# First feed-forward of a hybrid decoder layer: group 1 by seven products, the left combinations kind by kind, twelve modulation sums moved

## The chip, the cores and the metric

The kernel runs on one core of one Trainium2 chip. The metric is device time in microseconds for one execution, the median of several runs. A run's time is a little longer than the span of its profile, which goes from the first to the last instruction.

## The reference

One layer of a decoder on 1024 tokens of width 1024, all in f32: a feed-forward half-step, a mixer (a short convolution beside a diagonal state-space model), a second feed-forward half-step, and a final norm. Each of the three sub-layers is normed and modulated by vectors that come from a condition:

```python
c_act = jax.nn.silu(cond)
mod = c_act @ w_mod[l] + b_mod[l]
(sh1, sc1, g1, sh2, sc2, g2, sh3, sc3, g3) = jnp.split(mod, N_MOD, axis=-1)

h = modulate(rms_norm(x, ffn1_norm[l]), sh1, sc1)
x = x + 0.5 * g1[:, None, :] * swiglu(h, ffn1_w_gate[l], ffn1_w_up[l], ffn1_w_down[l])
...                        # mixer with sh2, sc2, g2; second feed-forward with sh3, sc3, g3
def swiglu(h, w_gate, w_up, w_down):
    return (jax.nn.silu(h @ w_gate) * (h @ w_up)) @ w_down
```

The hidden width of a feed-forward is 2816. `w_mod` is 1024 x 9216, so each of the nine modulation vectors takes eight sums over 128 x 1024 tiles of weights. The state-space model needs tables (powers and sines of its parameters, products with its B and C matrices) that depend on weights alone, not on x.

## The kernel before, in words

**Tiling.** Activations lie with the model width on the 128 partitions, as tiles of 128 x 512: eight width tiles k for each of two token halves h. A product of f32 accuracy is made from three matmuls of a rounded high part and a low part of each operand (`mm3`, line 315). A weight tile or an activation tile is split into its two parts by a cast on ACT (high) and a subtraction on DVE (low): `Weights.pump` for weights, `split_act` (line 328) for activations.

**Groups.** The 2816 hidden columns of the first feed-forward are worked in eleven groups of 256, named fa0 to fa10 in the profile. Each group computes silu(gate) * up for both token halves and keeps the result in DRAM (`kept`), and the down projection follows in chunks of four groups (fad0, fad1) and a last part of three groups (fald).

**Two ways to do a group.** Group 0 is interleaved with the norm at the start. Group 1 (`gate_up`, line 1317) is plain: two gate and two up weight tiles, each against eight width tiles and two halves. Groups 2 to 10 (`seven`, line 626) see a group as a 2 x 2 block product and do it with seven block products instead of eight, in the manner of Strassen and Winograd. Each of the seven takes one left block (A11, S1, S2, S4, S3, A12, A22, where A's rows are the token halves and the S are sums and differences of blocks, so 4 tiles of 128 x 512 each) and one right block (a weight, or a sum of weights). The products are accumulated in three PSUM banks B, C, A for the gate side and three for the up side; partial results are copied out of them by ACT and added by DVE between the products. Here a group's plain order of products is `SEVEN`.

**Weights.** `Weights` (line 108) streams weights through three raw buffers and a ring of four split tiles. The sums of weights are made in the raw buffers by DMAs issued from POOL that add a second block onto the first (`add`, line 165). `Weights.seven` (line 147) fixes in which order the seven right-hand tiles are made (granules) and in which order they are used.

**Left combinations.** `combos1` (line 1258) makes S1, S3, S2, S4 of the normed x once, in place in the x tiles, one k after another, and splits them. The split of S4 waits for `left_free`, which is set inside group 1, because its tiles take the place of A21, which plain group 1 still reads. When the combinations are done the x tiles are given back, and the tables' pools take their place.

**Side work and the clock.** A counter (`Clock`, line 57) ticks once per `mm3`, 0.68 us of TensorE. Every `period` ticks it takes one step of a queue of side work, `side1` (line 1283): the left combinations, then `ssm_base` (line 1024, the base of the tables, 35 steps), then `ssm_batch` (line 1165) for each of eight batches of tables. A batch reads parameters, builds its tables on DVE, runs small matmuls and transposes (kp and tp), and stores the tables by DMA. If side work isn't finished when group 10 begins, the rest is driven out at that place in the program; then the tables' pools are closed and x is loaded again into that space.

**Modulation sums.** After the start, 56 sums (`mod_tile`, line 459) are still to be made, each of one 512 KB load issued on SP and one DVE operation over 128 x 1024 (in the profile wm<-wm,cact). `MODS = (12, 12, 20, 12)` shares them out: 12 in group 1, 12 in batches 4 to 7 of the tables (`gate1`, line 1247, three in a batch), 20 in the last part of the down projection, 12 in the mixer. The loads go round a small ring: 2 buffers for those in the batches, and each sum starts the load of another.

**What sets the order.** The program's text gives each instruction its priority. A planner with costs of its own then lays out the queue of each engine, taking the first instruction in text order that it thinks is ready, and allotting buffers as they come free. So an instruction can be issued long before its place in the text. On the chip each queue runs in the planned order, and an instruction that waits holds up all that stands behind it on its engine. At the start alone the order is written out by hand.

Of the kernel before, what the change touches and what calls it, by code (L numbers as in the profile page):

```python
# [28 lines left out]
NGRP = NF // 2  # L29
# [2 lines left out]
CH = 16  # L32
TAU = 8

SEVEN_FROM = (2, 1)

CHUNKS = 2

# [2 lines left out]
NB = 8  # L41
# [78 lines left out]
class Weights:  # L120
# [23 lines left out]
    def plain(self, src):  # L144
        self.order.append(self.granule(self.source(src)))

    def seven(self, b, inner=()):

        b11, b12, b22, b21 = (b[q] for q in range(4))
        x = self.source(b11)  # L150
        got = [self.granule(x, b12)]
        self.order.append(got[0])
        for src in inner:
            self.plain(src)
        y = self.source(b12, b22)
        got += [self.granule(y, b11), self.granule(x), self.granule(y, b21)]
        got += [self.granule(self.source(src)) for src in (b22, b21)]
        got.append(self.granule(y))
        self.order.extend(got[q] for q in (2, 3, 4, 1, 5, 6))
# [62 lines left out]
def hymba_layer(ctx: ExitStack, tc, x_d, xt_d, wm1_d, wmod_d, gu1_d, gs1_d, ds1_d, wl1_d, win_d, wout_d, glu_d, gu2_d, gs2_d, wd2_d, ds2_d, wl2_d, cols_d, cond_d, lam_d, bc_d, out_d):  # L222
# [57 lines left out]
    def stream(gu, gs, wd, ds, wl, m):  # L280


        for g in range(m):
            plain([gu[2 * g], gu[2 * g + 1]])
        for g in range(m, NGRP):
            ws.seven(gs[g - m], [wd[:, q, :] for q in range(2)] if g == 1 else ())
        for c in range(CHUNKS):
            for p in range(2):
                ws.seven(ds[c, p])
        plain([wl[i] for i in range(wl.shape[0])])  # L290
# [332 lines left out]

    SEVEN = (("A11", "B"), ("S1", "C"), ("S2", "B"), ("S4", "C"), ("S3", "B"), ("A12", "A"), ("A22", "B"))

    def seven(name, between=None, kept=None, then=None):


        a_tiles, gate_, bank, t1, c1, u2 = {}, {}, {}, {}, {}, {}

        def copied(dst, b, side, nm):
            dst[side] = t2k(f"{name}{side}{nm}")
            A.copy(dst[side][:], bank[b, side][:])

        def add(dst, b, side):
            V.tensor_tensor(out=dst[side][:], in0=dst[side][:], in1=bank[b, side][:], op=ALU.add)

        def out(side, h, fi, src, t):
            if side == "g":
                A.activation(t[:], src[:], AF.Silu, scale=-1.0 if fi else 1.0)  # L640
                gate_[h, fi] = t
            elif kept is None:
                joined(t[:], src[:], gate_[h, fi][:], ALU.mult, fi == 1)
                a_tiles[fi, h] = split_act(t[:], f"{name}_{fi}_{h}a")
            else:
                keep(kept, f"A{h + 1}{fi + 1}", src[:], gate_[h, fi][:], ALU.mult, name, t[:], fi == 1)

        for n, (left, b) in enumerate(SEVEN):
            (w,) = ws.take()
            for half, side in enumerate("gu"):  # L650
                opens = (b, side) not in bank
                if opens:
                    bank[b, side] = ps(f"{name}{side}{b}")
                for k in range(4):
                    while len(blocks[left]) <= k:
                        clock.step()
                    mm3(bank[b, side][:], w, 4 * half + k, blocks[left][k], opens and k == 0, k == 3, more=not opens)
                if n == 0:
                    copied(t1, "B", side, "t1")
                elif n == 1:  # L660
                    copied(c1, "C", side, "c1")
                elif n == 2:
                    copied(u2, "B", side, "u2")
                elif n == 3:
                    add(u2, "C", side)
                    out(side, 0, 1, u2[side], u2[side])
                elif n == 4:
                    add(c1, "B", side)
                    out(side, 1, 1, c1[side], c1[side])
                elif n == 5:  # L670
                    add(t1, "A", side)
                    out(side, 0, 0, t1[side], t1[side])
                else:
                    if side == "g":
                        last = pools["first"].tile([P, HALF], F32, tag="first", name=f"{name}c21") if "first" in pools else acc_in_mov(f"{name}c21")
                    out(side, 1, 0, bank["B", side], last)
            ws.free()
            if n == 0 and between is not None:
                between()
            if then is not None:  # L680
                then(left)
        if kept is not None and kept.sums:
            keep_sums(kept, name)
            keep_last(kept, name)
        return a_tiles
# [479 lines left out]
    def ssm_batch(b):  # L1165
# [26 lines left out]
        bl = bt(f"bl{b}")  # L1192
        bl4 = bl[:, :512].rearrange("p (g n c) -> p g n c", g=GB, n=8)
        yield from comb(bl4, 8, (e1, e2), (bb[:, 0], bb[:, 1]), ALU.add, f"blt{b}")
        if b >= NB - 4:
            yield from gate1()

        def v3(a):
# [26 lines left out]
        tp = sm([P, 512], f"tp{b}")  # L1225
        for g in range(GB):
            T.transpose(tp[:, g * P : (g + 1) * P], bl[:, g * P : (g + 1) * P], ident[:])
        if b >= NB - 4:
            yield from gate1()
            yield from gate1()  # L1230
        kc = bt(f"kc{b}")
# [15 lines left out]
    def gate1():  # L1247

        if fetched:
            mod_tile(mod_home)  # L1250
            yield
# [1 line left out]
    def mod_home(name):  # L1253
        return mod_home.pool.tile([P, 1024], F32, tag="wm", name=name, bufs=2)[:]

    left_free = []

    def combos1():

        blocks.clear()  # L1260
        blocks.update(A11=act1[0][:4], A12=act1[0][4:], A22=act1[1][4:], S1=[], S2=[], S3=[], S4=[])
        for k in range(4):
            (t11, t21), (t12, t22) = x[k], x[4 + k]
            V.tensor_tensor(out=t22, in0=t22, in1=t21, op=ALU.subtract)
            blocks["S1"].append(split_act(t22, f"h1S1_{k}", "B"))
            yield
            V.tensor_tensor(out=t21, in0=t11, in1=t21, op=ALU.subtract)
            blocks["S3"].append(split_act(t21, f"h1S3_{k}", "B"))
            yield
            joined(t11, t22, t11, ALU.subtract, True)  # L1270
            blocks["S2"].append(split_act(t11, f"h1S2_{k}", "B"))
            yield
            joined(t12, t12, t11, ALU.subtract, True)
            yield
        while not left_free:
            yield
        for k in range(4):
            blocks["S4"].append(split_act(x[4 + k][0], f"h1S4_{k}", "A"))
            yield
        xp_open.close()  # L1280
        first_opened()

    def side1():
        yield from combos1()
        sb = side_open.enter_context(tc.tile_pool(name="sb", bufs=1, side="right"))
        with tc.tile_pool(name="sb1", bufs=1, side="right") as sb1:
            yield from ssm_base(sb, sb1)
# [26 lines left out]
        if d == KT - 1:  # L1314
            norm_into(act2, h, n2[h], 1, "h2")

    def gate_up(act, name, kept, last):

        afs = {}
        for fi in range(2):  # L1320
            if last and fi:
                wg, wu = ws.take(2)
                for h in (1, 0):
                    pg, pu = proj(wg, act[h], f"{name}g{fi}_{h}"), proj(wu, act[h], f"{name}u{fi}_{h}")
                    gu_keep(fi, h, pg, pu, afs, kept, name)
                    if h:
                        left_free.append(True)
                        clock.period = LAST_PERIOD
                ws.free(2)
                continue  # L1330
            (wg,) = ws.take()
            pg = [proj(wg, act[h], f"{name}g{fi}_{h}") for h in range(2)]
            ws.free()
            (wu,) = ws.take()
            for h in range(2):
                gu_keep(fi, h, pg[h], proj(wu, act[h], f"{name}u{fi}_{h}"), afs, kept, name)
            ws.free()

    movs["B"] = es1.enter_context(tc.tile_pool(name="movB1", bufs=12))
    LAST_PERIOD, BATCH_PERIOD = 2, 5.5  # L1340
    first_open = ExitStack()

    def first_opened():
        pools["first"] = first_open.enter_context(tc.tile_pool(name="first", bufs=1))

    MODS = (12, 12, 20, 12)

    share[0] = MODS[0]
    for _ in range(3):
        mod_fetch(mod_mov)  # L1350
    for i in range(MODS[0]):
        clock.after(2.5 * i + 3, lambda: mod_tile(mod_mov))
    clock.side.append(side1())
    clock.period = 3.5
    for g in range(1, SEVEN_FROM[0]):
        gate_up(act1, f"fa{g}", kept[g], g == SEVEN_FROM[0] - 1)
    clock.period = 4.5
    lefts = [{left: [] for left, _ in SEVEN} for _ in range(CHUNKS)]
    a_last = [{} for _ in LAST[0]]
    HOMES = dict(A11="A", S2="B", A12="A", S3="B", S1="B", A22="A", S4="A")  # L1360
# [12 lines left out]

    for g in range(SEVEN_FROM[0], NGRP):
        if g == NGRP - 1:
            while clock.side:
                clock.step()
            side_open.close()
            first_open.close()
            open_x(ctx)  # L1380
            load_x(range(2), (0, 2))
        if g == NGRP - 2:
            pools.pop("first")
        seven(f"fa{g}", kept=kept[g], then=(lambda left: fetch_chunk(0, left)) if g == NGRP - 1 else None)
    down7("fad0", lefts[0], 0, lambda left: fetch_chunk(1, left), lambda left: load_x(range(2), (1, 3)) if left == "A12" else None)
    down7("fad1", lefts[1], 0, fetch_last)
    clock.period = 4
# [456 lines left out]
```

## Time and profile before

| | |
|---|---|
| time, median of 3 runs | 1702.88 us (1699.06 to 1704.96) |
| time of the profiled execution | 1695.99 us |
| its span | 1694.2 us |
| TensorE busy / VectorE / ScalarE / GpSimd | 98% / 63% / 40% / 10% |
| group 1 (plain) begins / group 2 begins | 75.66 us / 119.18 us |
| group 10 begins / down chunk 0 begins | 442.03 us / 480.11 us |
| modulation loads | 56 of 512 KB, 6.6 us to landing |

In the profile PE is TensorE, DVE VectorE, ACT ScalarE, POOL GpSimd, and SPq the queue of SyncE, which issues most DMAs. An entry reads "result<-operands", with buffer numbers left out: h is an activation of the first norm, h1S a left combination, w a split weight, raw a loaded weight, wm a modulation weight, kp and tp the small products of a table batch, fa2uC the PSUM bank C of the up side of group 2. In brackets stand the idle time before an instruction and what ended it.

### The profile page before, as it was taken

Reading aid. Unit: us, or ns where it says so; the run is one execution under the profiler, and the core shown is the slowest. Engines: PE = TensorE matmul, PEld = TensorE weight load, DVE = VectorE, ACT = ScalarE, POOL = GpSimd, SP = SyncE. Lnnn points to the kernel's source line nnn. Section 1 sums busy time; section 2 is a strip of 40 time slices with the busy share of each in tenths; the row PEclk is TensorE's granted clock in tenths of the full one; section 3 lists DMA queues with packets and bytes.
Section 4 is the critical chain, followed back from the end, with each engine's and each line's share of the span. In section 5 each row is a group of like instructions: output and inputs, shape, how many; then the busy total and the mean of one; then the engine's idle time right before and its main releaser. Section 6 shows DMA issues by size and latency. Waiting matters only on the chain.

```text
span 1694.2 us, 20669 instructions
## 1 busy us (share of the span) xinstructions
PE 1664.0 (98%) x7545; PEld 1370.0 (81%) x7545; DVE 1063.2 (63%) x1572; ACT 670.3 (40%) x983; POOL 165.2 (10%) x203
## 2 busy tenths in 40 slices
PE   8999999999999999999999999999999999999997
PEld 5887878788878888788888778888888888888887
DVE  7976676776566767735666847856555655454454
ACT  7526333333454432332214416434444444322234
POOL 1001000001001102200000121000001001000003
PEclk9999999999999999999999999999999999999999
DMA  9557897887887768235753323557787777989812
GB/s 361 177 164 187 227 265 213 219 210 200 276 275 202 209 177 291 73 101 161 209 156 113 100 99 143 132 136 222 237 234 204 221 219 219 321 272 343 255 60 100
DMA packets 128552, 338.11 MB, mean 200 GB/s; under 512 B 22337, under 2 KB 37953, under 8 KB 127426
## 3 DMA queue, kind: packets, MB, share of 16 engines
q1 hardware_dynamic: 112898, 280.16, 47.7%
q0 software_dynamic: 15552, 56.63, 19.3%
q8 instruction: 59, 0.97, 0.2%
q14 instruction: 43, 0.35, 0.1%
HBM read 252.32 MB, written 76.02 MB: 194 GB/s over the span
## 4 chain that ended last, share of the span: by engine, by line
PE 80%; DVE 8%; DMA 7%; ACT 2%; issue 1%; SPq 1%; POOL 0%; DVEq 0%; POOLq 0%; ACTq 0%
PE fald L111 4%; DMA wm<-in_wmod 3%; PE p L111 3%; PE fbd_1B L111 3%; PE fbd_0B L111 3%; PE fb10d L111 2%; PE fad_0B L111 2%; PE fad_1B L111 2%; PE wo L111 2%; PE b L111 2%; PE u L111 2%; PE fad_1C L111 1%; DMA swx<-X 1%; PE fbd_1C L111 1%; PE fbd_0C L111 1%
## 5 line engine op out<-in xcount | busy, mean ns | idle before, releaser
L111 DVE TENSOR_TENSOR w<-raw,w 128x1024 fp32r<-128x1024 f32 x239 | 292.5, 1226 | 248.3 <-ACT w L111 237.2
L111 ACT CAST w<-raw 128x1024 fp32r<-128x1024 f32 x239 | 250.9, 1051 | 305.0 <-DMA raw<-in_ds 59.4
L166 POOL DMA_DIRECT2D raw<-in_gs x76 | 66.7, 878 | 753.5 <-DVE w L111 425.9
L111 DVE CUSTOM_DVE_ANT_0 wm<-wm,cact 128x1024 f32<-128x1024 f32 x56 | 75.7, 1374 | 38.6 <-DMA wm<-in_wmod 38.6
L166 POOL DMA_DIRECT2D raw<-in_ds x32 | 28.0, 875 | 284.4 <-DVE w L111 162.5
L111 PE MATMUL p<-h,w 128*128 128x512 f32 x192 | 49.4, 407 | 1.7 <-ACT h L111 1.5
L111 PE MATMUL wo<-oa,w 128*128 128x512 f32 x192 | 46.7, 399 | 2.2 <-ACT w L111 2.2
L111 PE MATMUL wo<-ob,w 128*128 128x512 f32 x192 | 45.7, 392 | 1.1 <-ACT ob L111 0.6
L111 PE MATMUL v<-h,w 128*128 128x512 f32 x192 | 46.0, 393 | 0.0
L111 PE MATMUL c<-h,w 128*128 128x512 f32 x192 | 46.0, 393 | 0.0
L111 PEld LDWEIGHTS wo<-oa,w 128*128 128x128 f32 x192 | 36.9, 193 | 10.5 <-ACT w L111 2.6
L111 PE MATMUL b<-h,w 128*128 128x512 f32 x192 | 45.1, 392 | 0.0
L111 PE MATMUL u<-h,w 128*128 128x512 f32 x192 | 44.7, 391 | 0.2 <-DVE h L111 0.2
L111 PEld LDWEIGHTS p<-h,w 128*128 128x128 f32 x192 | 35.7, 192 | 9.9 <-ACT h L111 2.0
L111 PEld LDWEIGHTS wo<-ob,w 128*128 128x128 f32 x192 | 35.7, 188 | 9.3 <-ACT ob L111 1.0
L111 PEld LDWEIGHTS u<-h,w 128*128 128x128 f32 x192 | 35.7, 188 | 8.3 <-DVE h L111 0.6
L111 PEld LDWEIGHTS b<-h,w 128*128 128x128 f32 x192 | 35.7, 188 | 7.3
L111 PEld LDWEIGHTS v<-h,w 128*128 128x128 f32 x192 | 35.5, 188 | 7.1
L111 PEld LDWEIGHTS c<-h,w 128*128 128x128 f32 x192 | 35.5, 188 | 7.0
L111 DVE SCALAR_TENSOR_TENSOR x<-fb10d,gate,x 128x512 f32<-128x512 f32 (+1 forms) x20 | 12.9, 643 | 24.4 <-PE fb10d L111 24.3
L111 PE MATMUL fb10d<-fb9lA,w 128*128 128x512 f32 (+1 forms) x120 | 25.6, 347 | 0.0
L111 DVE TENSOR_TENSOR X<-co,X 128x512 f32<-128x512 f32 x8 | 5.5, 693 | 31.5 <-DMA swx<-X 24.7
(1503 smaller groups left out, 3868.5 us busy)
## 6 DMA issues: line engine op xcount, KB each, us to landing
raw<-in_gs SPq DMA_DIRECT2D x76, 512.0 KB, 4.8
raw<-in_gs POOLq DMA_DIRECT2D x76, 512.0 KB, 6.4
wm<-in_wmod SPq DMA_DIRECT2D x56, 512.0 KB, 6.6
raw<-in_ds SPq DMA_DIRECT2D x32, 512.0 KB, 4.9
raw<-in_ds POOLq DMA_DIRECT2D x32, 512.0 KB, 7.6
mw<-in_wm SPq DMA_DIRECT2D x8, 1024.0 KB, 8.3
raw<-in_win SPq DMA_DIRECT2D x16, 512.0 KB, 4.3
raw<-in_gu SPq DMA_DIRECT2D x12, 512.0 KB, 9.8
```

Of the source, the lines that this page charges most:

```text
L111: r = getattr(self.engine, name)(*args, **kw)
L166: self.G.dma_start(out=r[:], in_=src, accum_op=ALU.add)
```

## The change

Group 1 is done by seven products like groups 2 to 10, but in its own order `SOON`: A11 and A12 first, then S1, S2, S4, S3, A22. `Weights.seven` gets a matching order of loads and uses (`soon`). The left combinations are made kind by kind (all four S1, then S2, S4, S3), with no wait for plain group 1. The sums of group 1 are gone from there: batches 2 to 7 of the tables now take four each, 24 in all. The periods of the side work change: 2 ticks from group 1's start, 4.5 as soon as the combinations are done; in the batches it stays at 5.5.

```diff
-SEVEN_FROM = (2, 1)
+SEVEN_FROM = (1, 1)
...
-    def seven(self, b, inner=()):
+    def seven(self, b, inner=(), soon=False):
         b11, b12, b22, b21 = (b[q] for q in range(4))
+        if soon:
+            x, y = self.source(b11), self.source(b12, b22)
+            z = self.source(b21)
+            got = [self.granule(x, b12), self.granule(y, b11), self.granule(z), self.granule(x), self.granule(y, b21)]
+            got += [self.granule(self.source(b22)), self.granule(y)]
+            self.order.extend(got[q] for q in (0, 2, 3, 4, 5, 1, 6))
+            return
...
+    SOON = [SEVEN[n] for n in (0, 5, 1, 2, 3, 4, 6)]
+
-    def seven(name, between=None, kept=None, then=None):
+    def seven(name, between=None, kept=None, then=None, order=SEVEN):
...
-        for n, (left, b) in enumerate(SEVEN):
+        for n, (left, b) in enumerate(order):
...
-                    while len(blocks[left]) <= k:
+                    while len(blocks.get(left, ())) <= k:
                         clock.step()
...
-        if b >= NB - 4:
+        if b >= 2:
             yield from gate1()
...
-        if b >= NB - 4:
+        if b >= 2:
+            yield from gate1()
             yield from gate1()
             yield from gate1()
...
     def combos1():
...
             blocks["S1"].append(split_act(t22, f"h1S1_{k}", "B"))
             yield
+        for k in range(4):
+            (t11, t21), (t12, t22) = x[k], x[4 + k]
             V.tensor_tensor(out=t21, in0=t11, in1=t21, op=ALU.subtract)
-            blocks["S3"].append(split_act(t21, f"h1S3_{k}", "B"))
-            yield
             joined(t11, t22, t11, ALU.subtract, True)
             blocks["S2"].append(split_act(t11, f"h1S2_{k}", "B"))
             yield
+        for k in range(4):
+            (t11, t21), (t12, t22) = x[k], x[4 + k]
             joined(t12, t12, t11, ALU.subtract, True)
-            yield
-        while not left_free:
+            blocks["S4"].append(split_act(t12, f"h1S4_{k}", "A"))
             yield
         for k in range(4):
-            blocks["S4"].append(split_act(x[4 + k][0], f"h1S4_{k}", "A"))
+            blocks["S3"].append(split_act(x[k][1], f"h1S3_{k}", "B"))
             yield
         xp_open.close()
         first_opened()
 
     def side1():
         yield from combos1()
+        clock.period = 4.5
...
-    def gate_up(act, name, kept, last):
...
-    LAST_PERIOD, BATCH_PERIOD = 2, 5.5
+    BATCH_PERIOD = 5.5
...
-    MODS = (12, 12, 20, 12)
-
-    share[0] = MODS[0]
-    for _ in range(3):
-        mod_fetch(mod_mov)
-    for i in range(MODS[0]):
-        clock.after(2.5 * i + 3, lambda: mod_tile(mod_mov))
+    MODS = (0, 24, 20, 12)
+
     clock.side.append(side1())
-    clock.period = 3.5
-    for g in range(1, SEVEN_FROM[0]):
-        gate_up(act1, f"fa{g}", kept[g], g == SEVEN_FROM[0] - 1)
-    clock.period = 4.5
+    clock.period = 2
...
-        seven(f"fa{g}", kept=kept[g], then=(lambda left: fetch_chunk(0, left)) if g == NGRP - 1 else None)
+        seven(f"fa{g}", kept=kept[g], order=SOON if g == 1 else SEVEN, then=(lambda left: fetch_chunk(0, left)) if g == NGRP - 1 else None)
```

More of the change, by code (lines that the diff above doesn't have):

```diff
@@ L285, in stream @@
         for g in range(m, NGRP):
-            ws.seven(gs[g - m], [wd[:, q, :] for q in range(2)] if g == 1 else ())
+            ws.seven(gs[g - m], [wd[:, q, :] for q in range(2)] if g == 1 and wd is not None else (), g == 1 and wd is None)
         for c in range(CHUNKS):
@@ L654, in seven @@
                 for k in range(4):
-                    while len(blocks[left]) <= k:
+                    while len(blocks.get(left, ())) <= k:
                         clock.step()
                     mm3(bank[b, side][:], w, 4 * half + k, blocks[left][k], opens and k == 0, k == 3, more=not opens)
-                if n == 0:
+                if left == "A11":
                     copied(t1, "B", side, "t1")
-                elif n == 1:
+                elif left == "S1":
                     copied(c1, "C", side, "c1")
-                elif n == 2:
+                elif left == "S2":
                     copied(u2, "B", side, "u2")
-                elif n == 3:
+                elif left == "S4":
                     add(u2, "C", side)
                     out(side, 0, 1, u2[side], u2[side])
-                elif n == 4:
+                elif left == "S3":
                     add(c1, "B", side)
                     out(side, 1, 1, c1[side], c1[side])
-                elif n == 5:
+                elif left == "A12":
                     add(t1, "A", side)
@@ L1254, in mod_home @@
         return mod_home.pool.tile([P, 1024], F32, tag="wm", name=name, bufs=2)[:]
-    left_free = []
     def combos1():
@@ L1315, in after1 @@
             norm_into(act2, h, n2[h], 1, "h2")
-    def gate_up(act, name, kept, last):
[L1319 to L1337, printed above, removed]
     movs["B"] = es1.enter_context(tc.tile_pool(name="movB1", bufs=12))
-    LAST_PERIOD, BATCH_PERIOD = 2, 5.5
+    BATCH_PERIOD = 5.5
     first_open = ExitStack()
```

## The prediction

> **What bounds the kernel now.** I read the page's busy shares and chain first, then a table of windows with one row for each group of the first feed-forward, then the waits of TensorE in that stretch.
>
> ```profile
> span 1694.2 us, 20669 instructions
> PE 1664.0 (98%) x7545; PEld 1370.0 (81%) x7545; DVE 1063.2 (63%) x1572; ACT 670.3 (40%) x983; POOL 165.2 (10%) x203
> PE 80%; DVE 8%; DMA 7%; ACT 2%; issue 1%; SPq 1%; POOL 0%; DVEq 0%; POOLq 0%; ACTq 0%
> ...
> L111 DVE TENSOR_TENSOR w<-raw,w 128x1024 fp32r<-128x1024 f32 x239 | 292.5, 1226 | 248.3 <-ACT w L111 237.2
> ```
>
> TensorE is busy 98% of the span and carries 80% of the chain, so matmuls taken out count in full unless a wait takes their place. The windows below go from the first matmul of group 1 to that of group 2, and so on; the one from 442.00 is group 10, the one from 480.11 the first down chunk. Columns: length, then busy us of PE, PEld, DVE, ACT, POOL, granted clock, DMA share, GB/s.
>
> ```profile
> 75.66:119.18 43.52, 43.52 (x194) 36.04 (x192) 30.73 (x70) 9.67 (x14) 3.61 (x36) 1.00 0.72 211
> 119.18:158.96 39.78, 38.96 (x169) 31.30 (x168) 29.25 (x67) 25.10 (x43) 3.53 (x4) 1.00 0.60 144
> 158.96:197.04 38.08, 38.08 (x169) 31.53 (x168) 20.03 (x30) 12.76 (x17) 3.52 (x4) 1.00 0.81 219
> 197.04:236.74 39.70, 38.79 (x170) 31.54 (x169) 30.06 (x45) 12.01 (x17) 3.52 (x4) 1.00 0.91 277
> 236.74:278.02 41.28, 41.28 (x193) 33.55 (x193) 31.50 (x58) 15.56 (x23) 3.52 (x4) 1.00 0.79 210
> 278.02:321.63 43.61, 41.83 (x193) 33.39 (x193) 32.39 (x57) 15.49 (x24) 3.53 (x4) 1.00 0.80 212
> ...
> 402.50:442.00 39.50, 39.50 (x181) 32.42 (x180) 21.73 (x31) 14.95 (x20) 3.54 (x4) 1.00 0.79 215
> 442.00:480.11 38.11, 38.11 (x169) 31.53 (x168) 21.52 (x29) 19.79 (x31) 3.52 (x4) 1.00 0.99 334
> 480.11:560.00 79.89, 76.52 (x328) 62.18 (x327) 55.86 (x75) 41.50 (x65) 7.04 (x8) 0.98 0.82 236
> ```
>
> ```profile
> PE fad_1C L111 <- ACT fad_1c L111: 2.9, 1, 2.9
> PE fa6gB L111 <- DVE fa6gc L111: 1.0, 1, 1.0
> PE fa4uB L111 <- DVE fa4uc L111: 0.8, 1, 0.8
> PE fa6uB L111 <- DVE fa6uc L111: 0.8, 1, 0.8
> ```
>
> A group by seven products without table batches takes 38.08 us (group 3). A batch adds its kp and tp matmuls: group 5 holds two and takes 41.28, so 1.60 each, with no wait. Against this, group 2 loses 39.78 - 38.08 = 1.70 us, group 4 1.62, group 6 43.61 - 41.28 = 2.33. These three and the losses in the first down chunk are all that the stretch has to give or to grow.
>
> **Group 1: fewer matmuls.** By plain products it has 192 matmuls, by seven 7 x 2 x 4 x 3 = 168.
>
> ```profile
> 75.66 11.04 PE L111 MATMUL fa1g<-h,w 128*128 128x512 f32 x48
> 113.74 5.60 PE L111 MATMUL fa1u<-h,w 128*128 128x512 f32 x24
> 119.18 2.88 PE L111 MATMUL fa2gB<-h,w 128*128 128x512 f32 x12
> ```
>
> It runs without a gap, 0.2267 us a matmul. 24 fewer are **-5.44 us**, and group 1 becomes a 38.08.
>
> What that group gets on the other engines: three more weight tiles to split (DVE 1.23 each by the page's group; ACT 1.0, two in 2.01 in a row below), six copies out of PSUM and six adds. For DVE that is 3.7 + 6 x 0.68 (an operation of that size, below) = 7.8 us more, but ten of the twelve modulation sums that leave lie inside its window, 12.3 us of its 30.73. All this lies beside 38 us of matmuls; if this cover were gone it would cost its own 7.8.
>
> **Left combinations.** The new order needs A11 at 75.66, A12 at 81.10, then S1 at 86.54, S2 at 91.98, S4 at 97.42, S3 at 102.86. Before, three of the four kinds are made during the start, in gaps:
>
> ```profile
> 57.64 1.66 ACT L111 CAST h1S<-x 128x512 fp32r<-128x512 f32 x3
> 66.01 2.01 ACT L111 CAST w<-raw 128x1024 fp32r<-128x1024 f32 x2
> ```
>
> ```profile
> 69.87 1.21 DVE L111 CUSTOM_DVE_ANT_0 wm<-wm,cact 128x1024 f32<-128x1024 f32 x1
> 83.71 0.68 DVE L111 TENSOR_TENSOR h1S<-x,h1S 128x512 fp32r<-128x512 f32 x1
> ```
>
> The twelfth tile is done at 84.4, behind four sums (from 69.87 on) that go away. Kind by kind the four S1 tiles come first, so they have some 15 us in hand, and S4 (its buffers come free when A21 is last read, at 75.66) has 20. The first weights are cast by 68. I cost this at **0**; the cover is A11 and A12, 10.9 us of matmuls, and without it the price would be the wait for S1.
>
> **Four accumulating DMAs on POOL** join the weights of group 1. One falls in the start, where the DMA engines are full up to 40 us and then idle:
>
> ```profile
> 20.00:40.00 20.00, 19.61 (x91) 15.43 (x90) 16.77 (x28) 17.13 (x27) 6.71 (x5) 0.94 0.96 391
> 40.00:60.00 20.00, 20.00 (x105) 16.50 (x104) 18.64 (x31) 13.22 (x21) 0.00 (x0) 1.00 0.36 116
> ```
>
> 512 KB at 391 GB/s is 1.3 us, the upper bound if it pushed the last first-norm modulation load; I take 0, because after 40 us two thirds of the DMA time is free. The others have 10 us (two products) between the slot that comes free and the use.
>
> **The table base** (sines, powers: 25.10 us of ACT in group 2 against 12.76 in group 3) follows the combinations, whose end is seen by the load of its parameters:
>
> ```profile
> 109.74 0.33 SPq L111 DMA_DIRECT2D lam<-in_lam  x1
> ```
>
> It can start some 25 us earlier, in group 1. There the PSUM copies on ACT meet it as they now do in group 2. So the 1.70 moves with it: **0**, between -1.7 (it fits between) and +1.7 (both groups hit).
>
> **The sums.** All 24 now stand in batches 2 to 7, four in each, where 12 stood in batches 4 to 7. The order in program text isn't the order of issue: the planner pulls a sum forward as soon as it thinks its load has landed.
>
> ```profile
> 189.85 1.23 DVE L111 CUSTOM_DVE_ANT_0 wm<-wm,cact 128x1024 f32<-128x1024 f32 x1 [2.80 <-DMA wm<-in_wmod]
> 216.70 1.23 DVE L111 CUSTOM_DVE_ANT_0 wm<-wm,cact 128x1024 f32<-128x1024 f32 x1 [5.55 <-DMA wm<-in_wmod]
> 221.61 1.23 DVE L111 CUSTOM_DVE_ANT_0 wm<-wm,cact 128x1024 f32<-128x1024 f32 x1 [0.40 <-DMA wm<-in_wmod]
> 225.63 1.23 DVE L111 CUSTOM_DVE_ANT_0 wm<-wm,cact 128x1024 f32<-128x1024 f32 x1 [2.78 <-DMA wm<-in_wmod]
> 230.64 1.23 DVE L111 CUSTOM_DVE_ANT_0 wm<-wm,cact 128x1024 f32<-128x1024 f32 x1 [0.84 <-DMA wm<-in_wmod]
> 242.70 1.23 DVE L111 CUSTOM_DVE_ANT_0 wm<-wm,cact 128x1024 f32<-128x1024 f32 x1 [0.92 <-DMA wm<-in_wmod]
> 313.38 0.29 DVE L111 TENSOR_TENSOR bb<-prm,qq 128x128 f32<-128x128 f32 x1 [3.59 <-DMA si_d<-rott]
> ```
>
> Twelve sums stand between 189.85 and 243.9, long before batches 4 to 7. In group 4 DVE is busy 30.06 us and waits 5.55 + 0.40 + 2.78 + 0.84 = 9.57 for their loads: 39.63 of 39.70, DVE was the bound there, and behind each waiting sum stand the adds that free PSUM (fa4uc, 0.8 on PE) and the next weight split. Two buffers go round through SP, which holds weight loads behind them. Another twelve make a second such group: **+1.62**. Bounds: 0 if they fall into gaps, and 14.3 us if all their waits come through to PE (9.57 x 12 / 8 for the same spacing, as eight to nine sums lie in group 4).
>
> **Thinner batches.** Group 6 loses 2.33 where DVE waits 3.59 for a table to leave its buffer, with batches 5 steps (27.5 ticks of 0.68 us, and 1.60) apart. From batch 2 on they come 9 steps apart, 35.3 us. Batches 0 to 2 stay dense and now meet sums; I take half of it back, **-1.17** (bounds -2.33 and 0).
>
> **The end of the tables.** Before: 35 steps of 4.5 ticks for the base and 52 of 5.5 for the batches, 443 of the 448 ticks of groups 2 to 9. After: from tick 34 of group 1, 34 + 157.5 + 64 x 5.5 = 543 of 504. Some 7 steps, nearly all of batch 7, are driven out in one go before group 10. There the loads of x wait for the tables' space:
>
> ```profile
> 423.54 1.05 PE L111 MATMUL kp<-cl,bl 128*16 128x128 f32 x8
> ```
>
> ```profile
> 426.24 5.27 SPq L111 DMA_DIRECT2D mk_d<-kc  x8
> 435.05 0.82 SPq L111 DMA_DIRECT2D x<-in_x  x2
> ```
>
> x goes out 11.5 us after batch 7's kp, 7 us ahead of group 10. With kp at the group's start it goes out 11.5 us into it, 18.5 later. Its first use is in the fourth product of the down stage, over 50 us on, so x isn't late itself; what is late next is the fetches of kept tiles, in a group whose DMA engines are at 0.99. Three 512 KB loads more in it are 1.57 MB / 334 GB/s = 4.7 us of DMA. I take a third, **+1.5**, since most fetches are issued 20 us and more ahead; bounds 0 and 4.7, and -5.9 if the new order happens to spare the down chunk its present losses (below).
>
> **Sum:** -5.44 + 0 + 0 + 1.62 - 1.17 + 1.5 = **-3.5 us**. The profiled execution took 1695.99 us (span 1694.2 and 1.8 around it), so 1692.5 for one like it; the median shown is 6.9 above it, and by that 1702.88 - 3.5 = **1699.4**.
>
> **A rule on waits.** The largest wait of the stretch ends here:
>
> ```profile
> 503.30 1.23 PE L111 MATMUL fad_1C<-fa1lS,w 128*128 128x512 f32 x3 [2.93 <-ACT fad_1c L111]
> 507.75 0.85 PE L111 MATMUL fad_0B<-fa1lS,w 128*128 128x512 f32 x3
> ...
> 562.16 0.84 PE L111 MATMUL fad_0B<-fa5lA,w 128*128 128x512 f32 x3
> ```
>
> Twelve matmuls between the first two took 4.45 us instead of 2.72: after 2.93 us of idling the clock was down, 1.73 more. The down chunk (from 480.11; two passes of 38.08 would end at 556.27, but the next chunk, the third row, begins at 562.16) loses 5.89 in all. The Trainium skill, "TensorE: Matmul & The Clock Gate", Part 1, says that the clock halves only after an idle window of about 3.4 us and needs as long a busy one to come back. By the row, a new wait of three microseconds costs nearly five; by that rule one of 2.93 may cost only itself, and the third rival below would then be at 1702.1 instead of 1703.8. The trace decides for the row.
>
> **Rivals.**
> - *Clean.* The sums hide, group 6 and half of the down chunk's losses go: -5.44 - 2.33 - 2.9 = -10.7, **1692.2**. For it: DVE has 17 to 18 us free in each of groups 3, 9 and 10. Against: the loads, not DVE time, were the limit in group 4.
> - *Slower: DVE runs over.* In groups 4 to 6 sums, batches 0 to 2 and group work meet; from where DVE's busy time and its waits for modulation loads pass the group's 38 to 41 us, each further wait is PE's. All waits of the second twelve through: -5.44 + 14.3 = +8.9, **1711.7**. For it: group 4 stood at 39.63 of 39.70 with one table batch around it; groups 5 and 6 are at 31.5 and 32.4 without a sum. Against: only 1.62 of 9.57 came through, and the planner counts DVE's time, if not the loads'.
> - *Late fetches.* The down chunk's 5.89 doubles: -5.44 + 1.62 - 1.17 + 5.89 = +0.9, **1703.8**. For it: 0.99 of DMA. Against: the slack of the fetches.
> - *The change doesn't do what it says*: a late S1 or weight gives the 5.44 back in group 1, **1702.9**. Only the 15 us in hand speak against it.
>
> **How the numbers follow.** 0.3% is 5.1 us, about what a measurement can tell from no change. Forecast 0.42 (same 0.33, faster 0.09, since its own range is 1696.5 to 1702), clean 0.32 (faster 0.30, same 0.02), DVE over 0.12 (slower 0.11), late fetches 0.10 (same 0.06, slower 0.04), group 1 stalls 0.04 (same 0.03, slower 0.01). Together faster 0.39, same 0.45, slower 0.16. The range goes from a little under the clean case to short of the DVE case: 1690.5 to 1706.5.
>
> **What would show it.** Group 1 right: from its first matmul to group 2's 38 to 40 us, PE never ending a wait for h1S. The base: ACT-heavy in that window. Sums: 24 of them closing by about 290 us, with one or two groups at 39.7. Tables: batch 7's kp in the first matmuls of group 10, x behind it. The prediction is wrong if group 1 stays above 41 us, if the groups 3 to 9 together lose over 8 us, or if the sums stay in batches 2 to 7 as written and cost nothing.

## The result, and the profile after

The changed kernel takes **1691.07 us** (median of six, 1685.42 to 1692.94) against 1700.97 us for the kernel before, run beside it (1698.63 to 1705.86): a ratio of 0.9932, 95% interval 0.9917 to 0.9946. A second set of the same two kernels gave 0.9929 (0.9909 to 0.9949). By these ratios the change saves 11.6 and 12.1 us (the medians lie 9.9 and 11.2 apart), over three times the 3.5 forecast. The profiled execution took 1691.52 us. The page of the changed kernel, its span and busy line:

```profile
span 1689.7 us, 20647 instructions
PE 1657.2 (98%) x7521; PEld 1364.8 (81%) x7521; DVE 1065.5 (63%) x1581; ACT 676.8 (40%) x992; POOL 169.4 (10%) x207
```

24 matmuls are gone, three weight splits and four POOL DMAs have come. The table of windows, changed kernel, again one row for a group: group 1 (75.92), 2, 4, 5, 6, 7, 10 (440.49), and the first down chunk (478.67). Columns as before: length, then busy us of PE, PEld, DVE, ACT, POOL, granted clock, DMA share, GB/s.

```profile
75.92:114.02 38.10, 38.10 (x169) 31.52 (x168) 30.62 (x67) 15.23 (x21) 4.66 (x37) 1.00 0.63 145
114.02:152.10 38.08, 38.08 (x169) 31.53 (x168) 22.62 (x54) 25.04 (x43) 3.53 (x4) 1.00 0.76 197
...
190.18:229.86 39.68, 39.68 (x181) 32.54 (x180) 26.07 (x40) 12.18 (x18) 3.54 (x4) 1.00 0.90 275
229.86:275.92 46.06, 41.67 (x193) 33.48 (x192) 33.55 (x60) 15.50 (x23) 2.75 (x4) 1.00 0.78 221
275.92:316.10 40.18, 40.10 (x181) 32.38 (x180) 30.89 (x56) 14.39 (x21) 4.33 (x5) 1.00 0.90 255
316.10:359.69 43.59, 41.52 (x182) 33.62 (x180) 34.04 (x60) 15.41 (x22) 3.53 (x4) 0.96 0.86 241
...
440.49:478.67 38.18, 38.18 (x172) 31.62 (x170) 22.45 (x34) 21.70 (x34) 3.53 (x4) 1.00 0.96 304
478.67:555.45 76.78, 76.71 (x338) 62.91 (x336) 54.64 (x76) 40.42 (x62) 7.04 (x8) 1.00 0.92 269
```

What TensorE waited for from group 1 to the end of the down projection, changed kernel (total, times, longest):

```profile
PE kp L111 <- DVE bl L111: 3.3, 1, 3.3
PE fa7gB L111 <- DVE fa7gc L111: 2.1, 1, 2.1
PE fa5gC L111 <- DVE w L111: 1.1, 1, 1.1
```

Three things are to be seen. Group 1 takes 38.10 us in place of 43.52 and waits for nothing. Groups 2 to 9 still lose time, now in 5, 6 and 7: 46.06 - 41.28 (two batches) = 4.78 in group 5, 40.18 - 39.68 = 0.50 and 43.59 - 39.68 = 3.91, 9.2 in all. And the down chunk, where the largest wait of the kernel before stood, is nearly free: 76.78 against 82.05, where 76.16 is what its matmuls need.

The table below is the same reading for each kernel run here: the length of group 1, what groups 2 to 9 lose against 38.08 us and 1.60 for each batch whose kp lies in them, what down chunk 0 loses against 76.16, and the measured ratio to the kernel before (95% interval).

| kernel | group 1 | groups 2-9 lose | chunk 0 loses | ratio |
|---|---|---|---|---|
| before | 43.52 | 5.5 | 5.9 | 1 |
| before, again | 43.52 | 9.1 | 7.5 | 1 |
| after | 38.10 | 9.2 | 0.6 | 0.9932 (0.9917-0.9946) |
| after, again | 38.14 | 5.5 | 0.2 | 0.9929 (0.9909-0.9949) |
| before, x behind fetches | 43.52 | 9.1 | 0.3 | 0.9967 (0.9951-0.9982) |
| after, x early | 38.22 | 6.2 | 7.0 | 0.9960 (0.9947-0.9974) |
| after, x early but behind | 38.09 | 5.3 | 0.0 | 0.9937 (0.9919-0.9955) |
| before, sums moved | 43.52 | 8.2 | 7.6 | 1.0021 (1.0010-1.0032) |
| after, half the sums | 38.21 | 2.6 | 2.0 | 0.9924 (0.9910-0.9938) |
| after, usual order | 38.08 | 13.5 | 2.7 | 0.9994 (0.9982-1.0006) |
| after, sums held | 38.11 | 0.6 | 14.3 | 0.9969 (0.9955-0.9984) |
| held, batches 1-6 | 38.13 | 0.0 | 9.4 | 0.9943 (0.9928-0.9957) |
| the same, x behind | 38.16 | 0.0 | 10.5 | 0.9948 (0.9934-0.9962) |
| the same, 5 ticks a step | 38.12 | 0.0 | 1.7 | 0.9898 (0.9882-0.9914) |

Each trace is of one execution out of several: with the sums held it is the slowest of twelve (1700.44 us, median 1694.12), in the usual order the fastest of twelve, and in the last row the fastest of five (1679.88, median 1684.27), so the losses of these rows are not those of a median run.

With the means of the two traces of each kernel: group 1 gives -5.4, groups 2 to 9 give 7.35 - 7.3 = 0, chunk 0 gives 0.4 - 6.7 = -6.3. Their sum, -11.7, is the measured gain, but the match is closer than the method: the whole spans of the same four traces lie only 9.6 apart on average, because what follows chunk 0 is 1.9 us longer in those of the changed kernel, and no run here says why. The same program loses 5.5 us in groups 2 to 9 in one execution and 9.2 in another, so a loss there of a few microseconds in a single trace says little.

### The profile page after: what moved, and what is told of

Same layout as the page of the kernel before. It is cut to its first block, busy times and chain, and to the rows that moved or that the text cites. A ratio compares the mean times of both kernels' runs of the same rounds, so it can differ in the third digit from the quotient of the medians.

```text
span 1689.7 us, 20647 instructions
## 1 busy us (share of the span) xinstructions
PE 1657.2 (98%) x7521; PEld 1364.8 (81%) x7521; DVE 1065.5 (63%) x1581; ACT 676.8 (40%) x992; POOL 169.4 (10%) x207
## 4 chain that ended last, share of the span: by engine, by line
PE 70%; DVE 7%; DMA 6%; issue 2%; SPq 1%; ACT 0%; POOL 0%; DVEq 0%; POOLq 0%; ACTq 0%
PE fald L111 4%; PE wo L111 3%; PE fad_0B L111 3%; PE fbd_0B L111 3%; PE fad_1B L111 3%; PE fbd_1B L111 3%; PE fb10d L111 2%; PE u L111 2%; PE b L111 2%; DMA wm<-in_wmod 2%; DMA swx<-X 2%; PE c L111 1%; DMA raw<-in_gs 1%; PE fad_0C L111 1%; PE fb0u L111 1%
## 5 line engine op out<-in xcount | busy, mean ns | idle before, releaser
L111 DVE TENSOR_TENSOR w<-raw,w 128x1024 fp32r<-128x1024 f32 x242 | 296.3, 1226 | 264.2 <-ACT w L111 263.9
L173 POOL DMA_DIRECT2D raw<-in_gs x80 | 70.6, 885 | 741.9 <-DVE w L111 454.0
```

Of the source, the lines that this page charges most:

```text
L111: r = getattr(self.engine, name)(*args, **kw)
L173: self.G.dma_start(out=r[:], in_=src, accum_op=ALU.add)
```

## The experiments

**Both kernels again**, without an edit, to see what one trace is worth.

> The kernel before once more, for a second trace of it. Both theories: group 1 43.5 us. Theory A (x loads): the first down chunk again takes about 82 us from its first product to that of the second chunk (5.9 lost), as its order of DMAs is fixed in the program. Theory B (chance): the losses of group 2 (1.7), group 4 (1.6), group 6 (2.3) and the down chunk (5.9) sit elsewhere or have other sizes this time.

> The changed kernel once more, timed and with a second trace. Expected ratio 0.993 to the kernel before. Theory A: the first down chunk takes 76 to 77 us again, and groups 5 and 7 lose 3 to 5 us each again. Theory B: the losses move.

Before: 1702.68 us. Its group 2 took 38.08 us where the first trace had 39.78, and its group 4 44.12 where that had 39.70. The down chunk lost 7.5 us, again the largest loss of one stage. After: 1688.38 us, ratio 0.9929.

**Where the down chunk's losses went.** In the kernel before the loads of x go out from 435.05 us on, the first of them ahead of the fetches of kept tiles and the last 15 us before the chunk begins; in the changed one they stand behind and among those fetches, the last of them 13.5 us into the chunk. The kernel before was given that order, with nothing else changed:

```diff
+ r = SP.dma_start(xt[k][h][:], x_d[...]); SP.follow(r, behind)
- load_x(range(2), (0, 2))        # ahead of group 10
+ # in group 10: (0, 2) behind the fetch for A11, later (1, 3) behind that for A22
```

> The kernel before with one edit: the eight loads of x are issued behind the fetches of kept tiles (four behind those of the first left block, four behind those of the last), as the changed kernel happens to issue them. Nothing of group 1, the sums or the tables is changed. Theory A (half of the gain comes from the x loads that no longer stand before the fetches): the first down chunk goes from 82 to 77 us, time -5.3 us, ratio 0.997. Theory B (the gain beyond the 24 matmuls comes from groups 2 to 9, the down chunk's loss is chance): ratio 1.000.

0.9967, as theory A had it: x alone is worth 5.6 us. The window of down chunk 0 in this kernel:

```profile
483.72:560.19 76.47, 76.44 (x338) 63.00 (x336) 54.67 (x74) 41.40 (x65) 7.04 (x8) 1.00 0.89 266
```

The reverse was tried on the changed kernel. Batches 5 to 7 run quicker, so that the tables end before group 10 and x goes out early again:

```diff
  for b in range(NB):
+     if b == 5: clock.period = 3.7
      yield from ssm_batch(b)
```

> The changed kernel with one edit: the period of side work is 3.7 ticks instead of 5.5 from table batch 5 on, so that the tables end some 25 ticks before group 10 as in the kernel before, and the x loads stand before the fetches again. Theory A: the first down chunk loses about 5 us again, ratio to the kernel before 0.996 instead of 0.993. Theory B: 0.993, or better where the last batch no longer falls on group 10.

0.9960, theory A's number, and the chunk loses 7.0 us again. Since that edit also makes the batches denser, the last run keeps the density and only orders x behind the fetches:

> The changed kernel with the last three batches at 3.7 ticks a step, as in the run that had x early and a ratio of 0.9960, but with the loads of x ordered behind fetches of kept tiles. Theory A (x ahead of the fetches was the whole loss of that run): down chunk 0 loses at most 1.5 us in place of 7.0, ratio 0.992 to 0.993. Theory B (the denser last batches, not x, were the loss): down chunk 0 still loses 5 us or more, ratio 0.996.

0.9937, and down chunk 0 is free. Theory A again. The chunk's window with x early (first fence), and with the same batches but x behind the fetches (second):

```profile
475.82:558.96 83.14, 79.00 (x337) 63.88 (x336) 57.60 (x78) 43.86 (x68) 7.03 (x8) 0.98 0.82 238
```

```profile
474.70:550.86 76.16, 76.16 (x337) 63.06 (x336) 54.44 (x75) 39.73 (x63) 7.02 (x8) 1.00 0.92 267
```

Density is not it; the place of x in SP's queue is. How it acts is seen on ACT's queue and SP's. First the kernel before:

```profile
496.72 0.58 ACT L111 COPY fad_0c<-fad_0C 128x512 f32<-128x512 f32 x1
499.91 0.62 ACT L111 CAST fa4lA<-fa4lA 128x512 fp32r<-128x512 f32 x1 [2.62 <-DMA fa4lA<-kept4X]
500.85 0.62 ACT L111 CAST fa5lA<-fa5lA 128x512 fp32r<-128x512 f32 x1 [0.32 <-DMA fa5lA<-kept5X]
...
502.67 0.58 ACT L111 COPY fad_1c<-fad_1C 128x512 f32<-128x512 f32 x1
...
464.92 0.95 SPq L111 DMA_DIRECT2D x<-in_x  x2
...
492.86 0.38 SPq L111 DMA_DIRECT2D fa5lA<-kept5X  x1
```

And the changed kernel:

```profile
496.41 0.62 ACT L111 CAST fa4lA<-fa4lA 128x512 fp32r<-128x512 f32 x1 [0.99 <-DMA fa4lA<-kept4X]
496.93 0.58 ACT L111 COPY fad_1c<-fad_1C 128x512 f32<-128x512 f32 x1
...
504.88 0.62 ACT L111 CAST fa5lA<-fa5lA 128x512 fp32r<-128x512 f32 x1 [4.25 <-DMA fa5lA<-kept5X]
...
450.10 1.86 SPq L111 DMA_DIRECT2D x<-in_x  x4
...
492.18 1.84 SPq L111 DMA_DIRECT2D x<-in_x  x2
...
500.18 0.38 SPq L111 DMA_DIRECT2D fa5lA<-kept5X  x1
```

With x out of the way the fetches for the next chunk (fa5lA and on) are issued early, 12.8 us into this chunk, and their casts are planned early too: three of them stand on ACT ahead of the copy fad_1c, for which TensorE waits. With x among the fetches fa5lA is fetched 21.5 us into the chunk, its cast stands behind the copy, and the copy runs 18.3 us into the chunk in place of 22.6 (496.93 - 478.67, 502.67 - 480.11). About half of these 4.3 us is the three casts (from 500.53 to 502.67); the rest is that fa4lA, ahead of the copy in both, is itself cast 2.1 us later, counted from the chunk's begin. The waits for DMA on ACT cost TensorE time here because a PSUM copy stands behind them.

The kernel before with x behind differs from the kernel before in nothing else, and shows the order of the changed kernel:

```profile
501.52 0.58 ACT L111 COPY fad_1c<-fad_1C 128x512 f32<-128x512 f32 x1
...
504.77 0.38 SPq L111 DMA_DIRECT2D fa5lA<-kept5X  x1
```

fa5lA is fetched 21.1 us into its chunk (it begins at 483.72), the copy runs at 17.8, and TensorE waits for nothing there. With x early in the changed kernel the casts of fa5lA to fa7lA stand ahead of fad_1c again, and TensorE waits 2.0 us for that copy and 1.6 for fad_0c.

**The sums.** Moved alone, in the kernel before (group 1 plain, no sums in it, two where one stood in the batches):

```diff
  def gate1():
      if fetched:
          mod_tile(mod_home)
+         mod_tile(mod_home)
          yield
- MODS = (12, 12, 20, 12)        # and the twelve of group 1
+ MODS = (0, 24, 20, 12)
```

> The kernel before with plain group 1, its twelve sums moved alone: gate1 makes two sums where it made one, so the steps of side work stay the same, and nothing is summed in group 1. The prediction's term: one more group that loses 1.6 us, ratio 1.001. Theory A (each dozen of sums costs what groups 4 to 6 lose): up to +4 us, 1.002. Theory B (hidden): 1.000, or a little less if the start or group 2 (1.7 lost in one trace, none in another) gains from 12 us of DVE work that leaves.

1.0021, theory A's number: 3.6 us slower (1.7 to 5.4). Its trace shows only half of that in this stretch (8.2 and 7.6 lost, 1.8 over the mean of the kernel before).

Half of the batch sums left out of the changed kernel (the vector g1 and four tiles of sc2 are constants instead of being computed), all steps kept:

```diff
+ del later[:12]; V.memset(gate[:, 0, :], 0.5); ...
-     mod_tile(mod_home)
+     if len(calls) % 2: mod_tile(mod_home)
```

> The changed kernel with twelve of its 24 batch sums left out (the gate vector of the first feed-forward and four of the eight tiles of the mixer's scale are set to constants instead; so this part of the computation is missing), every second call of gate1 making one, with the same steps of side work. Theory A (sums pulled forward hold DVE's queue in groups 4 to 7): the losses of groups 5 and 7 (4.3 to 4.8 and 1.2 to 3.9 us in the two traces) shrink by half or more, time -3 to -5 us against the changed kernel, ratio to the kernel before 0.990 to 0.991. Theory B (the sums lie in gaps; the table batches alone make these losses): 0.993.

0.9924, nearer to theory B: no gain that can be told from the changed kernel's 0.9932, though groups 2 to 9 lose only 2.6 us; the chunk loses 2.0, and what follows the chunk is 1.7 us longer in this trace than in those of the changed kernel. The wait of kp in group 5 is gone, however. In the changed kernel, on DVE and PE:

```profile
230.34 1.23 DVE L111 CUSTOM_DVE_ANT_0 wm<-wm,cact 128x1024 f32<-128x1024 f32 x1 [1.60 <-DMA wm<-in_wmod]
...
232.48 1.21 DVE L111 CUSTOM_DVE_ANT_0 wm<-wm,cact 128x1024 f32<-128x1024 f32 x1
...
237.57 1.21 DVE L111 CUSTOM_DVE_ANT_0 wm<-wm,cact 128x1024 f32<-128x1024 f32 x1
...
244.13 0.67 DVE L111 TENSOR_TENSOR bl<-bl,blt 128x512 f32<-128x512 f32 x1
...
244.95 1.03 PE L111 MATMUL kp<-cl,bl 128*16 128x128 f32 x8 [3.28 <-DVE bl L111]
```

And with half of the sums:

```profile
228.97 1.23 DVE L111 CUSTOM_DVE_ANT_0 wm<-wm,cact 128x1024 f32<-128x1024 f32 x1 [2.17 <-DMA wm<-in_wmod]
...
237.88 0.69 DVE L111 TENSOR_TENSOR bl<-bl,blt 128x512 f32<-128x512 f32 x1
...
241.23 1.05 PE L111 MATMUL kp<-cl,bl 128*16 128x128 f32 x8
```

Three sums and a wait for a load, 5.2 us of DVE, stand ahead of the bl that the batch's kp needs. The kp stands in PE's queue inside a product of the group, nine of its twelve matmuls done, and holds up the rest. With half of the sums one sum and its wait, 3.4 us, stand there; the kp comes 3.7 us sooner and waits for nothing. But bl itself comes 6.2 us sooner (237.88, 244.13), and the sums make only 1.8 of that: four adds of group 4 and a weight split, 3.8 us, stand ahead of bl in the one plan and behind it in the other. So the wait is one of DVE's order, in which the sums have a part; how large theirs is alone was not measured.

**The order of group 1.** The usual order, S1 second, in place of A12 second:

```diff
- seven(..., order=SOON if g == 1 else SEVEN, ...)
+ seven(..., order=SEVEN, ...)        # and the weights in the usual order
```

> The changed kernel with group 1 in the usual order of products and weights (A11, S1, S2, S4, S3, A12, A22) instead of A11, A12 first. S1 is then needed at 81.3 instead of 86.7 us, S2 at 86.7; in the second trace the splits of S1 end by 69 and those of S2 by 76. Theory A (the kinds are ready long before): group 1 takes 38.1 us all the same, ratio 0.993. Theory B (A11 and A12 first are what covers the combinations): group 1 takes 40 us or more, ratio 0.994 or above.

0.9994. Group 1 takes 38.08 us all the same, so the new order isn't needed as a cover for the combinations. What cost the time lies, in the trace, in groups 4 and 5. The whole plan has shifted: 20 sums are made before 240 us in place of 14, and those two groups lose 13.5 us (the largest wait 4.1, for an add that frees PSUM).

**Sums held.** Each sum is tied to the DVE instruction before it in the text, so that the planner cannot pull it forward:

```diff
  clock.period = BATCH_PERIOD
+ pools["mixed"] = False        # sums follow the DVE instruction before them
```

> The changed kernel with each batch sum held in DVE's queue behind the operation that stands before it in the program, so that sums are made in batches 2 to 7 as written (some 35 us apart in fours) and are not pulled forward. Theory A (pulling forward makes the wait of 2.7 to 3.3 us for batch 1's kp in group 5): groups 5 and 7 run free, -4 to -6 us against the changed kernel, ratio 0.990. Theory B: the same 0.993, the waits only move to where three sums stand in a row.

Groups 2 to 9 are free (0.6 lost), but the down chunk loses 14.3 us and the ratio is 0.9969, above what either theory expected. The loss was taken for SP's queue standing behind modulation loads of batch 7, and three runs tested it: the held sums one batch earlier, four in each of batches 1 to 6; then x behind the fetches as well; then 5 ticks a step in place of 5.5.

```diff
- if b >= 2: yield from gate1()            # four in each of batches 2 to 7
+ if 1 <= b <= 6: yield from gate1()
```

> The changed kernel, with its 24 batch sums held at their places in the text (each behind the DVE instruction before it) and moved one batch earlier: four in each of batches 1 to 6 and none in 7. Theory A (where the plan puts the sums makes the losses of groups 2 to 9; the 14.3 us that the down chunk lost with held sums came from modulation loads of batch 7 that held up SP's queue at group 10): groups 2 to 9 lose at most 2 us, down chunk 0 at most 3, ratio 0.989 to 0.9905. Theory B (losses only wander: what the groups spare, the down chunk pays, because held sums make the tables late whatever batch they are in): groups free, down chunk 0 loses 8 us or more, ratio 0.994 to 0.997.

> As the run before it, and the loads of x are also ordered behind fetches of kept tiles by the text, as in the kernel before with x behind. Theory A: no more than 1 us from the run before it if x already went out late there; if x went out early there, 5 to 6 us less in down chunk 0, ratio 0.989 to 0.9905 either way. Theory B: 0.994 to 0.997 as well, since the late weights and not x make the loss.

> As the run before it, with 5 ticks for a step of the batches in place of 5.5, so that batch 7 ends some 20 us before group 10. Theory A: if tables driven out at group 10 still cost something in down chunk 0, this ends it, 0 to 3 us less; the groups stay within 3 us of free, since 3.8 DVE-heavy batches more in the same time are covered; ratio 0.988 to 0.990. Theory B (denser batches bring the losses back into groups 4 to 7): 5 us or more lost there, ratio 0.992 or more.

The first two stay at 0.9943 and 0.9948, with 9.4 and 10.5 us lost in the chunk: theory A was wrong about modulation loads, of which none stands there. SP's queue and ACT in the first of them (group 10 begins at 429.14):

```profile
439.17 0.47 SPq L111 DMA_DIRECT2D raw<-in_ds  x1
...
447.19 5.77 SPq L111 DMA_DIRECT2D mk_d<-kc  x8
...
453.68 0.38 SPq L111 DMA_DIRECT2D raw<-in_ds  x1
...
471.26 1.05 ACT L111 CAST w<-raw 128x1024 fp32r<-128x1024 f32 x1 [12.35 <-DMA raw<-in_ds]
```

By the queue it is the stores of batch 7 itself. Driven out inside group 10, they stand between two loads of down weights, which go out 14.5 us apart (439.17 and 453.68): SP waits 3.9 us of this for a table that isn't made yet and is busy with the stores for most of the rest. The second and third load of down weights go out 24.6 and 30.5 us into the group, in the changed kernel 14.0 and 19.4. With 5 ticks a step the stores go out 2 us into group 10 (from 430.8) and no longer 18, and the loads of down weights follow one another 4.6 us apart:

```profile
432.79 5.99 SPq L111 DMA_DIRECT2D mk_d<-kc  x8
...
440.40 0.34 SPq L111 DMA_DIRECT2D raw<-in_ds  x1
...
442.34 2.56 SPq L111 DMA_DIRECT2D x<-in_x  x4
445.00 0.56 SPq L111 DMA_DIRECT2D raw<-in_ds  x1
```

Then the groups stay free and the chunk loses 1.7 us in the trace. This kernel takes **1684.27 us** (1679.88 to 1686.47), ratio **0.9898 (0.9882 to 0.9914)**, faster than both kernels. Theory B, that what the groups spare is paid later, fell with it. That the stores are the cause is read from the queue and borne out by this run; it moves all batches, not those stores alone, and the shares of late weights and of late kept tiles in the 9.4 us were not measured apart. Why the first run with held sums loses more, 14.3 us, stays open: there the same eight stores begin only 7.6 us into group 10, but a modulation load stands with them in SP's queue.

## Why the prediction was right or wrong

**Group 1, -5.44: right.** 43.52 to 38.10.

**Left combinations, 0: right**, and with more in hand than thought: even with S1 second nothing waits. **POOL's DMAs, 0:** right, group 1 begins 0.26 us later in the first pair of traces and 0.06 sooner in the second.

**The table base, 0: right, by a wrong reading.** It was to start in group 1 and to carry the 1.70 us of group 2 along. Its parameters do come sooner:

```profile
91.45 0.33 SPq L111 DMA_DIRECT2D lam<-in_lam  x1
```

That is 18 us sooner, not 25, and its ACT work still lies in group 2 (25.04 there). Yet group 2 takes 38.08 with it, and in the second trace of the kernel before too. The 1.70 stood in one execution and not in the others, so it is no cost of the base.

**Sums +1.62 and thinner batches -1.17: right in sum, wrong in mechanism.** Together +0.45 was forecast, 0 was measured. The forecast took a group 4 in which DVE was the bound, and a second such group after the change. Neither is stable: group 4 of the kernel before lost 1.5 in one execution (the 1.62 of the forecast ends its window 0.16 us into group 5) and 6.0 in another (44.12 - 38.08; no batch's kp lies in it), and in the changed kernel, where it holds one batch, it is free (39.68). The losses that the traces show are where TensorE meets something late on DVE: a batch's kp, fixed in PE's queue, whose bl stands behind sums and adds, or an add that frees PSUM, or a weight split. The 24 sums didn't close by 290 us: eight stand between 305 and 350. By the prediction's own test (groups 3 to 9 lose over 8 us) it fails in one trace, with 9.2, and passes in the other, with 5.5. Moved alone the sums cost 3.6, over twice the forecast. In the change they cost less where they then stand, or the thinner batches give as much back: these were never tried alone, so which of the two it is stays open.

**x late, +1.5: the step that failed.** Its facts were right: x went out 9.6 us into group 10 (450.10 - 440.49), 11.5 forecast, behind a kp of batch 7 at 439.1. Its price had the wrong sign: the chunk gains 6.3, and x behind the fetches alone, in the kernel before, is worth 5.6 (3.1 to 8.3). Such a gain was only named as the far bound (-5.9), as something that might happen and with no mechanism, so that the bound came true is luck. It priced the bytes of x in group 10, where the DMA share went down to 0.96, and overlooked that SP's order decides when kept tiles are fetched and cast, and that these casts stood ahead of a PSUM copy. The row was in sight: the largest wait of the stretch was for fad_1c, on an engine busy 53% of that window, which asks what stood ahead of that copy.

**Rivals.** *Clean* (1692.2) has the time, and half of the reason: all of the down chunk's losses go, not half, but groups 2 to 9 keep theirs. *DVE over* did not come; it would have needed more than one wait of 3.28 us. *Late fetches* did not come in the changed kernel, but a loss of that kind is real: 9.4 to 14.3 us where the stores of batch 7 slid further into group 10, though not in proportion to how far. The changed kernel lies between two edges, x ahead of the fetches and tables too far behind.

**The rule on waits.** The forecast took from one row that a wait of three microseconds halves the clock. These runs show that it may or may not. The same wait in two kernels whose TensorE instructions are the same up to group 10, first the kernel before again, then that with x behind, PE's row and the windows around it:

```profile
231.52 5.46 PE L111 MATMUL fa4gB<-h,w 128*128 128x512 f32 x12 [3.14 <-DVE fa4gc L111]
...
232.00:236.00 4.00, 4.00 (x11) 3.08 (x10) 4.00 (x8) 0.97 (x2) 0.19 (x1) 0.50 0.98 170
```

```profile
231.44 3.01 PE L111 MATMUL fa4gB<-h,w 128*128 128x512 f32 x12 [3.18 <-DVE fa4gc L111]
...
232.00:236.00 4.00, 4.00 (x19) 3.13 (x18) 4.00 (x8) 0.91 (x1) 0.27 (x1) 1.00 0.99 177
```

After 3.14 us of idling the clock is at 0.50 and twelve matmuls take 5.46 us; after 3.18 it is at 1.00 and they take 3.01. The Trainium skill, "TensorE: Matmul & The Clock Gate", Part 1, says that activity is judged over a free-running window of about 3.4 us. These rows fit a window that runs on by itself: whether a wait is caught would then depend on where it falls, which no trace here shows directly. They don't fit the rule that the prediction quoted from the same part of the Trainium skill, by which the clock falls only after an idle window of about 3.4 us: here it fell after 3.14. The measured rows decide.

In the changed kernel itself the kp of group 5 waited 3.28 us in one trace, and the clock stayed at 1.00 (243 to 247 us); in the other it waited 2.74 us, the clock was 0.66 over the same stretch, and the twelve matmuls of the group's next product (fa5gB) took 3.77 us in place of 2.90.

## What to carry to other kernels

A transfer's place in a queue can matter more than its bytes: before pricing a load that moves, look at what is issued sooner or later because of it, and whether a PSUM copy stands behind the casts of that. Where a planner sets the queues, a loss in a single trace that no full engine explains may belong to the plan or to chance; take a second trace before pricing a step by it. And side work that is driven out at a deadline should end in time for it: here half a tick a step decided over some 8 us.

## What the runs showed of the hardware

A wait's price on TensorE isn't fixed: 3.14 us of idling cost 2.45 us more (5.46 - 3.01) than 3.18 did, with the granted clock at 0.50 in the one and 1.00 in the other. In two executions of the changed kernel the shorter wait, 2.74 us against 3.28, was the one that slowed what followed. So a part of the spread from one execution of a kernel to the next can come from the same wait, caught by the clock or not; how large a part was not measured.
